# Third four of experts moved up, later down products behind their own up products, branch and row loads ahead of the last four

## Chip, cores, metric

One core of one Trainium2 chip. The metric is the device time of one execution in microseconds; three executions of the kernel before took 1126.81, 1130.20 and 1132.19 us (median 1130.2).

## The reference, cut to what matters

The program is one step of a two-layer backbone over 384 tokens of 1024 channels (128 context tokens, 256 latent ones). Each layer mixes tokens (convolution, windowed attention, spatial gating, one output projection) and then channels; each half ends in a LayerNorm. The change lies in the channel half, a mixture of experts in which every token takes 2 of 32 experts:

```python
gate = sum(one_hot(expert_id, 32) * top_w[..., None], axis=1)
hid = silu(einsum('td,edf->tef', t, w1)) * einsum('td,edf->tef', t, w3)
hid = hid * gate[..., None]
y = einsum('tef,efd->td', hid, w2)          # per expert 1024 -> 128 -> 1024
x = layer_norm(ALPHA * x + g2 * y, ln2_g, ln2_b)
```

## The kernel before, in words

`mixer` runs the token half, `moe` the channel half: `experts` (L1347), then `ln2` (L1679), once per layer. The 32 experts are taken in eight fours, `q` = 0 to 7. The 768 (token, expert) pairs are sorted by expert; matrix products with one-hot matrices (`gather_mm`) put the tokens' rows in that order, in three thirds of 256 places (`J` = 0, 1, 2; the third covers the later experts, the third four among them), and `evac` (L1356) copies a third from PSUM into `xT`.

For a four, `windows(q)` (L1367) copies 32 places for each of the four experts (ScalarE) and two further windows for experts with more rows (VectorE; the *second rows*). `ups(q, kqs)` (L1510) multiplies them with the up weights in four quarters `kq`; each quarter first copies the weights of the second rows' experts into `hv` (`copies`, L1392; two of three by VectorE, the third by ScalarE; two buffers) and ends in `self.done()`, which lets SP issue a later load into the freed buffer. `hidden` (L1420) applies SiLU on ScalarE and a product on VectorE, `hidden_T` (L1428) transposes the result on TensorE. `down(q, hT)` (L1466) makes the down products in three groups: two halves `z` = 0, 1 of the columns for the first rows, then both halves for the second rows. ScalarE scales `z` = 0 and the second rows by the gates, VectorE `z` = 1, and POOL writes the results into `y_d` in DRAM by one indirect DMA for the first rows (tile `ys`, two buffers) and one for the second rows (tile `ys2`, **one** buffer, so the second rows' scaling of the next four waits until this write has landed). The products go into the two PSUM banks of tag `sc`. Behind each write POOL does a piece of `affine`.

The gates and targets of these writes come from `gates` (L1201) and `slots` (L1279): some 25 small VectorE operations and twelve products. `overflow` (L1604) is a branch that runs only if an expert has more rows than the windows hold; on the given inputs it is not taken, but every engine loads `most` into a register and branches. `load_yy` (L1671) reads `y_d` back (three loads of 1 MB, a raw buffer each). The last four's down products (`down_keep`, L1482) stay in SBUF and are added up in token order by products with one-hot matrices (L1581, L1583); `ln2` adds the rows read back (L1691, first addition on PSUM at L1732) and normalizes.

Weights come in loads of 1 MB on SP's DMA queue: per four, four for the up products (32 per layer in ten buffers: tag `raw`, six, and `wx`, four) and two for the down products (`load_w2`, four buffers; issued behind the `down` that frees them). So a layer's fours load 48 MB.

The order on an engine named in `manual_schedule` is that of the code: VectorE, ScalarE and TensorE in the first block (L1515), TensorE alone in the second (L1546). Elsewhere a planner orders ScalarE, VectorE, POOL and SP by its own estimate of when each instruction is ready. It does not move instructions past the branch.

Of the kernel before, what the change touches and what calls it, by code (L numbers as in the profile page):

```python
# [8 lines left out]
F32 = mybir.dt.float32  # L9
# [11 lines left out]
D = 1024  # L21
NP, NS, T = 128, 256, 384
NT = 3
# [3 lines left out]
NQUAD = 8  # L27
# [52 lines left out]
class Kern:  # L80
# [1266 lines left out]
    def experts(self, l):  # L1347
        nc, mo, ep, tc = self.nc, self.mo, self.ep, self.tc
# [18 lines left out]
        def windows(q, ns=range(6)):  # L1367

            w = win[q]
            for n in ns:  # L1370
                at = first[4 * q + n] if n < 4 else more[q, n - 4]
                o, i_ = w[:, :, n * 32:(n + 1) * 32], xT[:, :, bass.ds(at, 32)]
                if n < 4:
                    self.act(o, i_, AF.Copy)
                else:
                    nc.vector.tensor_copy(o, i_)
            return w
# [42 lines left out]
        def hidden(ps):  # L1420

            pv = ps[:, 0:384].rearrange("p (h m f) -> p h m f", h=3, m=2)
            hid = ep.tile([128, 3, 64], F32, tag="hid", name="hid", bufs=1)
            self.act(hid, pv[:, :, 0, :], AF.Silu)
            nc.vector.tensor_tensor(hid, hid, pv[:, :, 1, :], op=ALU.mult)
            return hid
# [39 lines left out]
        def down(q, hT):  # L1466
            ys = self.eq.tile([128, D], F32, tag="ys", name="ys", bufs=2)
            yv = ys.rearrange("p (h z c) -> p h z c", h=2, z=2)
            for po, z in down_mm(q, hT):
                if z == 0:  # L1470
                    self.act(yv[:, :, 0, :], po.rearrange("p (h c) -> p h c", h=2), AF.Copy, scale=self.gate[:, 0, q:q + 1])
                elif z == 1:
                    nc.vector.tensor_scalar(yv[:, :, 1, :], po.rearrange("p (h c) -> p h c", h=2), self.gate[:, 0, q:q + 1], None, op0=ALU.mult)
                    scatter(self.y_d, ys, self.dst[:, 0, q:q + 1], 2 * T)
                else:
                    y2 = self.eq.tile([128, 512], F32, tag="ys2", name="ys2", bufs=1)
                    self.act(y2, po, AF.Copy, scale=self.gate[:, 1, q:q + 1])
                    scatter(self.y_d.rearrange("t (h c) -> (t h) c", h=2), y2, self.dst[:, 1, q:q + 1], 4 * T)
            for z in range(2):
                self.load_w2(l, 2 * q + z + 4)  # L1480
# [23 lines left out]
        w0 = ExitStack()  # L1504
# [5 lines left out]
        def ups(q, kqs):  # L1510
            for kq in kqs:
                up(ps[q], q, kq, win[q])

        ps = {}
        with tc.manual_schedule(engines={e.engine for e in (nc.vector, nc.scalar, nc.tensor)}):  # L1515

            for z in range(4):
                evac(0, z, "AAAV"[z])
            whos(0)
            windows(0)  # L1520
            ps[0] = self.bank("mm")
            ups(0, (0,))
            for z in range(4):
                evac(1, z, "AVAV"[z])
            ups(0, (1, 2, 3))
            windows(1)
            V.tensor_scalar(self.mid[:, 2, :], self.mid[:, 0, :], 1024.0, None, op0=ALU.add)
            ps[1] = self.bank("mm")
            ups(1, (0,))
            for i in range(NT):  # L1530
                self.onehot(oh[2, i], xT[:, i, 512:768], 2, i)
            self.gate_exp(self.logit)
            hid = hidden(ps[0])
            ups(1, (1,))
            hT = hidden_T(hid)
            ups(1, (2, 3))
            self.second_slots()
            whos(1)
            self.gates()
            for i in range(NT):  # L1540
                for part in (True, False):
                    self.gather_mm(oh, (2,), i, part)
        w0.close()
        self.eq = self.eqs.enter_context(tc.tile_pool(name=f"eq{l}", bufs=1, reuse_waits="tile"))

        with tc.manual_schedule(engines={nc.tensor.engine}):  # L1546
            self.slots()
            hid = hidden(ps[1])
            for z in range(4):
                evac(2, z, "AVAV"[z])  # L1550
            wn = self.hp.tile([128, 2, 8, 192], F32, tag="H", name="win")
            win += [wn[:, q % 2] for q in range(2, NQUAD)]
            windows(2)
            down(0, hT)
            for q in range(2, NQUAD):
                ps[q] = self.bank("mm")
                ups(q, (0, 1))
                hT = hidden_T(hid)
                ups(q, (2, 3))
                hid = hidden(ps[q])  # L1560
                if q < NQUAD - 1:
                    windows(q + 1)
                down(q - 1, hT)
            q, hT = NQUAD - 1, hidden_T(hid)
        self.ahead = self.NRAW
        self.overflow(l)
        self.load_yy(l)

        oT = [ep.tile([128, T], F32R, tag="hv", name="oT", bufs=2), self.eq.tile([128, 2, T], F32R, tag="ys", name="oT", bufs=2)]
        oT = [oT[0], oT[1][:, 0, :], oT[1][:, 1, :]]  # L1570
# [33 lines left out]
    def overflow(self, l):  # L1604
        nc, a, mo, ep, tc = self.nc, self.a, self.mo, self.ep, self.tc
        most = nc.values_load(self.most[0:1, 0:1], min_val=0, max_val=T + CAP + 6 * CAP * T)
        with tc.If(most > 2 * CAP):
            wo = self.wrp.tile([128, 2048], F32, tag="wr", name="wo")
            part = lambda c, n: wo[:, c:c + NT * n].rearrange("p (i e) -> p i e", i=NT)
# [26 lines left out]
            with tc.For_i(0, NQUAD, 1) as it:  # L1636
                nc.vector.tensor_copy(ixc, ix[:, :, bass.ds(it * 4, 4)])
                nc.vector.tensor_copy(gwc, gw[:, :, bass.ds(it * 4, 4)])
                w = [self.wx.tile([128, 2048], F32, tag="wx", name="w_ov") for _ in range(4)]
                for h in range(4):  # L1640
                    nc.sync.dma_start(w[h], a["w13"][bass.ds(it * 2 + (l * NHALF + h // 2), 1), h % 2].rearrange("o p c -> p (o c)"))
                w2 = [self.rawp.tile([128, 2048], F32, tag="raw", name="w2_ov") for _ in range(2)]
                for z in range(2):
                    nc.sync.dma_start(w2[z], a["w2"][bass.ds(it * 2 + (l * NHALF + z), 1)].rearrange("o p c -> p (o c)"))
                for e in range(4):
                    for i in range(NT):
                        ps = self.bank("mm")
                        for k in range(8):
                            c = e * 512 + k % 2 * 256
                            nc.tensor.matmul(ps[:, 0:256], tT[i][:, k * 128:(k + 1) * 128], w[k // 2][:, c:c + 256],  # L1650
                                             start=k == 0, stop=k == 7)
                        pv = ps[:, 0:256].rearrange("p (h m f) -> p h m f", h=2, m=2)
                        hid = ep.tile([128, 2, 64], F32, tag="hid", name="hidov", bufs=1)
                        self.act(hid, pv[:, :, 0, :], AF.Silu)
                        nc.vector.tensor_tensor(hid, hid, pv[:, :, 1, :], op=ALU.mult)
                        pt = self.bank("ms")
                        nc.tensor.transpose(pt[:, 0:128], hid.rearrange("p h f -> p (h f)"), self.ident)
                        hT = wo[:, 256:384]
                        nc.vector.tensor_copy(hT, pt[:, 0:128])
                        yo = wo[:, 1024:1024 + D]  # L1660
                        yv = yo.rearrange("p (h z c) -> p h z c", h=2, z=2)
                        for z in range(2):
                            po = self.bank("sc")
                            nc.tensor.matmul(po, hT, w2[z][:, e * 512:(e + 1) * 512], start=True, stop=True)
                            nc.vector.tensor_scalar(yv[:, :, z, :], po.rearrange("p (h c) -> p h c", h=2), gwc[:, i, e:e + 1], None, op0=ALU.mult)
                        nc.gpsimd.indirect_dma_start(
                            out=self.y_d, out_offset=bass.IndirectOffsetOnAxis(ap=ixc[:, i, e:e + 1], axis=0),
                            in_=yo, in_offset=None, bounds_check=2 * T - 1, oob_is_err=False)


    def load_yy(self, l):  # L1671
        nc = self.nc
        self.yy = []
        for i in range(NT):
            t = self.rawp.tile([128, 2, D], F32, tag="raw", name="yy")
            nc.sync.dma_start(t, self.y_d.rearrange("(c t) d -> t c d", c=2)[i * 128:(i + 1) * 128])
            self.yy.append(t)

    def ln2(self, l, ps):  # L1679
        nc, a, sm = self.nc, self.a, self.sm  # L1680
# [292 lines left out]
```

## Time and profile before

| | us |
|---|---|
| median of three executions | 1130.2 |
| the profiled execution, its own time | 1127.33 |
| its span, first to last instruction | 1125.6 |
| TensorE busy | 1011.2 |
| VectorE busy | 810.7 |
| ScalarE busy | 417.4 |
| POOL busy | 269.7 |

Busy times say little of a stage. The views used below are a table of stretches (busy time of each engine, granted TensorE clock as a share of full speed, share and rate of the DMA engines), the instructions of one engine in order of time (start, duration, engine, line, operation, out<-in, shape, count, in brackets the idle time before and what ended it), the DMA issues of a stretch with the time to landing, and the groups by line. Engines: PE is TensorE, PEld its weight loads, DVE VectorE, ACT ScalarE; a q marks an engine's sequencer. All times are from the start of the span. The experts of the first layer run from about 430 to 556 us, those of the second 545 us later.

### The profile page before, as it was taken

The numbers are of one execution on the slowest core, as the hardware profiler recorded it, in microseconds if no ns is written. First come the engines' busy times: TensorE is split into PE (matmuls) and PEld (weight loads), VectorE is DVE, ScalarE is ACT, GpSimd is POOL, SyncE is SP. The second block draws the span as 40 slices with busy tenths as digits, with TensorE's granted clock in tenths as the row PEclk, the third lists the DMA queues.
The fourth block names the chain that finished last, engine by engine and source line by source line (L and its number), as shares of the span: only waits on it lengthen the run. The fifth ranks groups of instructions, "written<-read, shape, count | busy, mean of one in ns | idle before, by whom it ended". The sixth has DMA issues, their size and how long they took to land. (4 is left out here: it accounts for less than half of the span.)

```text
span 1125.6 us, 20806 instructions
## 1 busy us (share of the span) xinstructions
PE 1011.2 (90%) x8182; PEld 840.7 (75%) x8182; DVE 810.7 (72%) x1530; ACT 417.4 (37%) x753; POOL 269.7 (24%) x232
## 2 busy tenths in 40 slices
PE   7999999999999999776689998999999999778673
PEld 5898978877999988433259897788999998754322
DVE  4399999965446986762569999997834587777437
ACT  4324254434333324341163443445532341434221
POOL 0001431221100510333244043114111025013335
PEclk9999999999999989897989999999999999989888
DMA  9967668447436667799585756773223666689955
GB/s 358 412 241 257 266 217 294 178 163 270 151 112 246 259 262 293 303 420 403 219 315 201 280 217 233 251 290 127 110 94 132 224 244 229 227 317 416 419 204 194
DMA packets 55101, 282.75 MB, mean 251 GB/s; under 512 B 8060, under 2 KB 12284, under 8 KB 27857
## 3 DMA queue, kind: packets, MB, share of 16 engines
q1 hardware_dynamic: 49632, 270.01, 63.1%
q0 software_dynamic: 5360, 11.29, 2.7%
q8 instruction: 69, 1.13, 0.4%
q14 instruction: 40, 0.32, 0.1%
HBM read 262.13 MB, written 24.71 MB: 255 GB/s over the span
## 5 line engine op out<-in xcount | busy, mean ns | idle before, releaser
L97 PE MATMUL ps_mm<-hThi,wr 128*128 128x384 f32 x672 | 229.9, 343 | 4.4 <-ACT hThi L102 2.3
L110 DVE TENSOR_TENSOR wr<-w_raw,wr 128x1024 fp32r<-128x1024 f32 x124 | 162.2, 1309 | 92.4 <-ACT wr L102 92.3
L98 PE MATMUL ps_mm<-hTlo,wr 128*128 128x384 f32 x672 | 228.0, 340 | 0.6 <-DVE hTlo L441 0.4
L99 PE MATMUL ps_mm<-hThi,wr 128*128 128x384 f32 x672 | 227.5, 339 | 0.6 <-DVE wr L110 0.6
L102 ACT ACTIVATE wr<-w_raw 128x1024 fp32r<-128x1024 f32 x140 | 147.5, 1055 | 68.1 <-PE ps_mm L99 37.8
L505 DVE SCALAR_TENSOR_TENSOR cacc<-pad,par,cacc 128x399 f32<-128x399 f32 x240 | 169.2, 705 | 4.2
L97 PEld LDWEIGHTS ps_mm<-hThi,wr 128*128 128x128 f32 x672 | 127.1, 189 | 18.2 <-issue 4.0
L98 PEld LDWEIGHTS ps_mm<-hTlo,wr 128*128 128x128 f32 x672 | 127.1, 189 | 6.3 <-DVE hTlo L441 2.5
L99 PEld LDWEIGHTS ps_mm<-hThi,wr 128*128 128x128 f32 x672 | 127.2, 189 | 2.5 <-DVE wr L110 0.9
L110 POOL TENSOR_TENSOR wr<-w_raw,wr 128x1024 fp32r<-128x1024 f32 x10 | 24.5, 2447 | 201.6 <-ACT wr L102 201.2
L1458 POOL DMA_INDIRECT y_d<-ys,dst x28 | 28.4, 1016 | 172.3 <-DVE hv L1400 73.3
L1446 PE MATMUL ps_sc<-w,hidT 128*32 128x512 f32 x256 | 43.1, 766 | 28.6 <-ACT ys L102 21.9
L1415 PE MATMUL ps_mm<-hv,win 128*32 128x128 f32 x1024 | 46.4, 277 | 9.2 <-DVE hv L1400 7.8
L1400 DVE COPY hv<-w_raw 128x512 f32 x60 | 41.9, 737 | 16.6 <-PE ps_mm L1415 10.8
L1415 PEld LDWEIGHTS ps_mm<-hv,win 128*32 128x32 f32 x1024 | 35.8, 112 | 22.7 <-DVE hv L1400 12.0
L1409 PE MATMUL ps_mm<-w_raw,win 128*32 128x256 f32 x640 | 47.8, 391 | 3.5 <-ACT win L102 3.5
L219 PE MATMUL ps_ms<-w_raw,cT 128*32 128x512 f32 x320 | 48.7, 612 | 1.4 <-DMA w_raw<-in_wada 1.4
L102 ACT ACTIVATE gate<-ps_mm 128x384 f32<-128x384 f32 x40 | 19.6, 490 | 81.6 <-PE ps_mm L99 80.5
L1446 PEld LDWEIGHTS ps_sc<-w,hidT 128*32 128x32 f32 x256 | 8.2, 123 | 45.8 <-ACT ys L102 32.9
L911 POOL TENSOR_TENSOR rtmp<-sc,lb 128x1024 f32<-128x1024 f32 x4 | 9.8, 2478 | 121.8 <-DMA lb<-in_ln 121.8
L842 POOL TENSOR_TENSOR merged<-merged,gate 128x384 f32<-128x384 f32 x16 | 18.1, 1135 | 87.0 <-DVE gate L841 87.0
L102 ACT ACTIVATE win<-xT 128x256 f32 x64 | 21.5, 409 | 37.6 <-PE ps_mm L1409 30.2
(505 smaller groups left out, 2355.7 us busy)
## 6 DMA issues: line engine op xcount, KB each, us to landing
w_raw<-in_wst SPq DMA_DIRECT2D x68, 1024.0 KB, 6.4
w_raw<-in_wada SPq DMA_DIRECT2D x48, 1024.0 KB, 5.4
w_raw<-in_w SPq DMA_DIRECT2D x40, 1024.0 KB, 10.7
w<-in_w SPq DMA_DIRECT2D x32, 1024.0 KB, 12.3
w_x<-in_w SPq DMA_DIRECT2D x24, 1024.0 KB, 11.8
bias<-in_bias SPq DMA_DIRECT2D x8, 768.0 KB, 7.6
y_d<-zero SPq DMA_DIRECT2D x2, 3072.0 KB, 15.1
yy<-y_d SPq DMA_DIRECT2D x6, 1024.0 KB, 7.1
```

Source lines behind the costliest of these rows:

```text
L97: mm(out, whi, xhi, start=first, stop=False)
L98: mm(out, whi, xlo, start=False, stop=False)
L99: mm(out, wlo, xhi, start=False, stop=last)
L102: return self.nc.scalar.activation(out, in_, f, **k)
L110: (eng or self.nc.vector).tensor_tensor(lo, x, hi.bitcast(F32), op=ALU.subtract)
L219: nc.tensor.matmul(ps[32 * t:32 * t + 32, :], self.cT[:, 2 * kp + k, :], w[:, t * 512:t * 512 + 512], start=(kp == 0 and k == 0), stop=(kp ...
L505: nc.vector.scalar_tensor_tensor(acc, pad[:, j:j + W], w, acc, op0=ALU.mult, op1=ALU.add)
L1400: nc.vector.tensor_copy(hv[:, i, :], src)
L1409: nc.tensor.matmul(ps[e * 32:(e + 1) * 32, 0:256], x[:, k, e * 32:(e + 1) * 32], w[:, e, kk, :], start=k == 0, stop=k == 7, skip_group_che ...
L1415: nc.tensor.matmul(ps[t * 32:(t + 1) * 32, 256:384], x[:, k, 128 + i * 32:160 + i * 32], hv[:, i, kk, h * 128:(h + 1) * 128], start=False, ...
L1446: nc.tensor.matmul(po[e * 32:(e + 1) * 32, :], hT[:, e * 32:(e + 1) * 32], w2[:, e, :], start=True, stop=True)
L1458: ins = nc.gpsimd.indirect_dma_start(out=view, out_offset=bass.IndirectOffsetOnAxis(ap=dst, axis=0), in_=rows, in_offset=None, bounds_chec ...
```

## The change

- The third four (`q` = 2) goes into the first block: the SiLU of the second four directly behind its up products, then after the last third's `gather_mm` the copies `evac(2)` and `windows(2)`, and all of `ups(2)`. `gates` and `slots` come behind it; in the second block `down(0)` and `down(1)` follow each other.
- `down(3)` and `down(4)` both follow `ups(4)`; from then on `down(q)` follows the up products of its own four, where it followed those of the next.
- `overflow` and `load_yy` stand ahead of `ups(7)`. The buffers of the rows read back are allotted before the branch, whose body borrows them. `ahead`, the number of up loads in flight, stays at ten until behind `ups(7)`.

```diff
             ups(1, (2, 3))
+            hid1 = hidden(ps[1])
             self.second_slots()
             whos(1)
-            self.gates()
             for i in range(NT):
                 for part in (True, False):
                     self.gather_mm(oh, (2,), i, part)
-        w0.close()
-        self.eq = self.eqs.enter_context(tc.tile_pool(name=f"eq{l}", bufs=1, reuse_waits="tile"))
-
-        with tc.manual_schedule(engines={nc.tensor.engine}):
-            self.slots()
-            hid = hidden(ps[1])
             for z in range(4):
                 evac(2, z, "AVAV"[z])
             wn = self.hp.tile([128, 2, 8, 192], F32, tag="H", name="win")
             win += [wn[:, q % 2] for q in range(2, NQUAD)]
             windows(2)
+            ps[2] = self.bank("mm")
+            ups(2, (0, 1))
+            hT1 = hidden_T(hid1)
+            ups(2, (2, 3))
+            self.gates()
+            w0.close()
+            self.eq = self.eqs.enter_context(tc.tile_pool(name=f"eq{l}", bufs=1, reuse_waits="tile"))
+            self.slots()
+
+        last = NQUAD - 1
+        with tc.manual_schedule(engines={nc.tensor.engine}):
+            hid = hidden(ps[2])
+            windows(3)
             down(0, hT)
-            for q in range(2, NQUAD):
+            down(1, hT1)
+            for q in range(3, last):
                 ps[q] = self.bank("mm")
                 ups(q, (0, 1))
-                hT = hidden_T(hid)
+                if q < 5:
+                    hT = hidden_T(hid)
                 ups(q, (2, 3))
                 hid = hidden(ps[q])
-                if q < NQUAD - 1:
-                    windows(q + 1)
-                down(q - 1, hT)
-            q, hT = NQUAD - 1, hidden_T(hid)
-        self.ahead = self.NRAW
+                windows(q + 1)
+                if q < 5:
+                    down(q - 1, hT)
+                if q >= 4:
+                    down(q, hidden_T(hid))
+
+        self.yy = [self.rawp.tile([128, 2, D], F32, tag="raw", name="yy") for _ in range(NT)]
         self.overflow(l)
         self.load_yy(l)
+        with tc.manual_schedule(engines={nc.tensor.engine}):
+            ps[last] = self.bank("mm")
+            ups(last, range(4))
+            q, hT = last, hidden_T(hidden(ps[last]))
+        self.ahead = self.NRAW
```

`overflow` takes its up weights from the three `yy` buffers and one more `raw` buffer, its down weights from two `wx` buffers; `load_yy` no longer allots.

## Rows read from the trace of the kernel before

**Rows 1.** Table of stretches, layer 0; columns in the first line

```profile
core 0: us, PE busy (x) PEld busy (x) DVE busy (x) ACT busy (x) POOL busy (x), PEclk, DMA share, GB/s
443.00:457.00 14.00, 9.21 (x88) 8.67 (x80) 9.85 (x37) 4.53 (x12) 0.00 (x0) 0.83 0.83 349
...
485.00:500.00 15.00, 11.17 (x214) 6.36 (x214) 9.15 (x17) 4.54 (x11) 5.56 (x5) 1.00 1.01 420
...
507.00:530.00 23.00, 14.43 (x189) 6.51 (x193) 6.56 (x16) 3.78 (x7) 7.67 (x5) 0.72 1.00 408
```

**Rows 2.** SP in order of time, layer 0

```profile
442.37 1.58 SPq L332 DMA_DIRECT2D w_x<-in_w  x2
...
459.33 2.08 SPq L342 DMA_DIRECT2D w<-in_w  x2
...
549.81 1.42 SPq L1676 DMA_DIRECT2D yy<-y_d  x3
```

**Rows 3.** DMA issues, 443.5 to 444 and 459.2 to 460 us; last: us to landing

```profile
w_x<-in_w SPq DMA_DIRECT2D x1, 1024.0 KB, 12.8
...
w<-in_w SPq DMA_DIRECT2D x1, 1024.0 KB, 4.9
```

**Rows 4.** Gates and slots, layer 0, DVE and PE in order of time

```profile
449.02 0.17 DVE L1205 TENSOR_REDUCE se<-ex 128x3 f32<-128x12 f32 x1 [1.69 <-issue]
...
454.63 2.77 PE L1304 MATMUL ps_ms<-V,RO 128*128 128x96 f32 x12 [4.79 <-ACT win L102]
```

**Rows 5.** ACT in order of time, layer 0, second rows' scaling among others

```profile
520.86 0.63 ACT L102 ACTIVATE hv<-w 128x512 f32 x1 [4.64 <-DMA w<-in_w]
...
521.39 0.67 ACT L102 ACTIVATE ys<-ps_sc,gate 128x512 f32<-128x512 f32 x1
...
538.52 0.69 ACT L102 ACTIVATE ys<-ps_sc,gate 128x512 f32<-128x512 f32 x1 [0.82 <-DMA y_d<-ys,dst]
...
545.07 0.69 ACT L102 ACTIVATE ys<-ps_sc,gate 128x512 f32<-128x512 f32 x1 [5.86 <-DMA y_d<-ys,dst]
```

**Rows 6.** Line 1458, writes into y_d, both layers

```profile
DMA to landing us min/median/max: 2.5/8.5/10.5
```

**Rows 7.** PE in order of time, layer 0, from the sixth four's down products

```profile
524.85 1.93 PE L1446 MATMUL ps_sc<-w,hidT 128*32 128x512 f32 x8 [0.81 <-ACT ys L102]
...
529.37 1.72 PE L1409 MATMUL ps_mm<-w_x,win 128*32 128x256 f32 x16
...
532.76 0.33 PE L1430 MATMUL ps_ms<-con,hid 128*128 128x128 f32 x1
...
535.90 1.04 PE L1446 MATMUL ps_sc<-w,hidT 128*32 128x512 f32 x8
...
539.70 1.07 PE L1453 MATMUL ps_sc<-hv,hidT 128*32 128x256 f32 x16 [0.88 <-DVE ys L1473]
...
544.15 3.60 PE L1446 MATMUL ps_sc<-w,hidT 128*32 128x512 f32 x16 [2.86 <-PEq L1607]
...
551.27 0.50 PE L1583 MATMUL ps_tp<-ysk,oT 128*128 128x512 f32 x1 [0.29 <-DVE ysk L1494]
```

**Rows 8.** Group by line, both layers: product of hidden

```profile
L1425 DVE TENSOR_TENSOR hid<-hid,ps_mm 128x192 f32<-128x192 f32 x16 | 5.6, 351 | 10.9 <-ACT hid L102 10.8
```

**Rows 9.** Line 1607, the branch, both layers: ns min/median/max, first and last start

```profile
L1607 SPq EVENT_SEMAPHORE  x14: 17/17/17, 538.2 to 1083.4; - x14
...
L1607 PEldq COMPARE_BRANCH  x2: 3342/3381/3420, 540.4 to 1085.8; - x2
```

**Rows 10.** DVE in order of time, layer 0, LayerNorm

```profile
555.59 0.69 DVE L1732 TENSOR_TENSOR x<-ps_tp,yy 128x512 f32<-128x512 f32 x1
...
558.53 1.75 DVE L1691 TENSOR_TENSOR yy<-yy 128x512 f32<-128x512 f32 x1
560.20 2.28 DVE L1701 SCALAR_TENSOR_TENSOR x<-r,x 128x1024 f32<-128x1024 f32 x1
...
567.36 1.22 DVE L1701 SCALAR_TENSOR_TENSOR x<-r,x 128x1024 f32<-128x1024 f32 x1
```

More of the change, by code (lines that the diff above doesn't have):

```diff
@@ L1606, in overflow @@
         most = nc.values_load(self.most[0:1, 0:1], min_val=0, max_val=T + CAP + 6 * CAP * T)
+        spare = self.rawp.tile([128, 2048], F32, tag="raw", name="w_ov")
+        w = [t.rearrange("p c d -> p (c d)") for t in self.yy] + [spare]
+        w2 = [self.wx.tile([128, 2048], F32, tag="wx", name="w2_ov") for _ in range(2)]
         with tc.If(most > 2 * CAP):
@@ L1638, in overflow @@
                 nc.vector.tensor_copy(gwc, gw[:, :, bass.ds(it * 4, 4)])
-                w = [self.wx.tile([128, 2048], F32, tag="wx", name="w_ov") for _ in range(4)]
                 for h in range(4):
                     nc.sync.dma_start(w[h], a["w13"][bass.ds(it * 2 + (l * NHALF + h // 2), 1), h % 2].rearrange("o p c -> p (o c)"))
-                w2 = [self.rawp.tile([128, 2048], F32, tag="raw", name="w2_ov") for _ in range(2)]
                 for z in range(2):
@@ L1672, in load_yy @@
         nc = self.nc
-        self.yy = []
         for i in range(NT):
-            t = self.rawp.tile([128, 2, D], F32, tag="raw", name="yy")
-            nc.sync.dma_start(t, self.y_d.rearrange("(c t) d -> t c d", c=2)[i * 128:(i + 1) * 128])
-            self.yy.append(t)
+            nc.sync.dma_start(self.yy[i], self.y_d.rearrange("(c t) d -> t c d", c=2)[i * 128:(i + 1) * 128])
     def ln2(self, l, ps):
```

## The prediction

> **What bounds the kernel now.** I read the table of stretches first. Between 485 and 500 us the DMA engines' share is 1.01 at 420 GB/s, and it is 1.00 from 507 to 530 [rows 1]: no engine is as full, so most of the experts' time is the stream of weights, and a 1 MB load costs 1.049 MB / 420 GB/s = 2.5 us. Changing the order of products there pays nothing. Three places of a layer aren't of that kind.
>
> *The hole at the front.* From 443 to 457 the share is only 0.83 [rows 1]. SP issues two up loads at 442.37, then nothing until down weights at 459.33 [rows 2]. The later of the two takes 12.8 us, so lands at 456.4; the down load takes 4.9 and lands at 464.2 [rows 3]. Without a gap it would land at 458.9: **5.3 us of stream are lost**, since SP waits for `down(0)`, and that for gates and slots (VectorE from 449.02, TensorE's L1304 at 454.63 after waiting 4.79) [rows 4].
>
> *The chain behind the last up weights but one.* The down weights of the sixth four land at 520.8; ScalarE copies `hv` from them at once [rows 5]. The DMA binds up to here and no further: SP's first record behind its wait for the last loads is at 538.2 [rows 9], while the first addition of `ln2` waits until 555.59 [rows 10]. In between, TensorE runs the rest of `down(5)` from 524.85, `ups(7)` from 529.37, `down(6)` from 535.90, the branch, then `down_keep` from 544.15 [rows 7]. Beside it runs a second chain: the second rows' scalings on ScalarE at 521.39, 538.52 and 545.07 (a fourth at about 530, as the spacing of 8.5 asks) each wait for the previous write to land [rows 5]; then the last write, then SP's reading back at 549.81 [rows 2]. Both chains end within a few us of each other, at 555.59.
>
> *LayerNorm*, 13.0 us from 555.59 to 568.58, the end of its last sum (567.36 + 1.22) [rows 10].
>
> **The change part by part**, for one layer; the second repeats the first 545 us later. No bytes, products or branches are added or dropped.
>
> *Third four moved up.* Its up products free buffers, so four up loads now follow at 456.4 without waiting for gates. Behind them the down loads still wait for `down(0)`, now behind `ups(2)`, gates and slots. `ups` cost 6.0 (529.37 to 535.90 less 0.52 of transposes, judged by the 0.33 of one [rows 7]), and I add 2.3 for `evac` and `windows` ahead of them, about half the wait of 4.79 [rows 4]: 8.3. L1304 comes at 463, the load is issued at 467.6 and lands at 472.5. Gapless it would be 456.4 + 5 x 2.5 = 468.9, so 3.6 stay lost of 5.3: **-1.7**. Bounds: -5.3, if slots come 3.6 earlier than that; +2.4, if the wait of 4.79 comes whole and VectorE's gates start late by as much as their chain lasts (5.6, 449.02 to 454.63), 4.1 beyond my sum.
>
> *`down` of neighbouring fours back to back* (0 and 1, 3 and 4). The second's second rows wait for the first's write through the one `ys2`: 8.5 by the median landing [rows 6]. ScalarE's later window copies stand behind that. In the streaming stretch TensorE is busy 11.17 of 15 us, ScalarE 4.54 [rows 1]: one such wait is covered by the stream, since ten up loads are ahead. Taken at 0; without that cover up to 8.5, once.
>
> *`down(6)` behind its own up products, and ahead of the branch and `ups(7)`.* TensorE's order after the landing at 520.8 becomes: rest of `down(5)`, 4.5 (524.85 to 529.37); `ups(6)`, 6.0; waiting for `hidden` and transposes, which before lay between quarters, 1.9 (0.52, three elementwise steps at about 0.35 [rows 8], handoffs); `down(6)` 3.8 (535.90 to 539.70); the last second-row products and branch, 4.45 (539.70 to 544.15); `ups(7)` 6.0 and again 1.9; from `down_keep` to the last L1583 of the first token tile 7.6 before (544.15 to 551.77), less 1.5, since its 16 products took 3.60 where twice eight should take 2 x 1.04 [rows 7] with no standstill ahead of them: 6.1. Sum 34.65, against 555.59 - 520.86 = 34.7, which before held 3.8 of waiting for the rows read back: **0**. Bounds: `down(5)` 3.0 and `down(6)` 2.1 where no bank is waited for (-3.2); `down(5)` whole at 8.6 (520.8 to 529.4), `down_keep` still 7.6 (+5.6).
>
> *Branch.* It takes 3.34 to 3.42 us on TensorE's sequencer [rows 9], and stays. The Trainium skill ("Advanced Engine Details and Errata", Control Flow Timing) gives about 108 ns for a compare-and-branch; by it the step would be some 3.2 us cheaper per layer. No row supports that, and the measurement decides. New is what waits at the branch: SP for outstanding loads (538.2 [rows 9]), POOL for its writes. `ups(7)`'s copies on ScalarE and VectorE stand behind their own branches.
>
> *Rows read back.* They move past the last up products but not past SP's wait for all loads: issue at about 537 to 541, in place of 549.81 [rows 2]. Three loads, landing over the next 10 us, beside `ups(7)` and `down_keep`: hidden. What they postpone on SP is the next layer's first tiles, which before stood behind them as well. Uncovered they would cost what they cost now. The pair sums on VectorE (1.75 each, L1691) then run before the first addition, where before two stood inside `ln2`, and the last sums fall from 2.28 toward 1.22 without the traffic beside them [rows 10]: of 13.0 us I take off one pair, 1.75, and 1.06: **-2.8**. Bounds: 0, and both pairs, -3.5.
>
> Sum per layer -1.7 + 0 - 2.8 = -4.5; two layers **-9.0**. The profiled execution took 1127.33, 2.9 below the median of three; 1130.2 - 9.0 = **1121.2**. About 0.5% (5.65 us) is what a measurement of this kernel tells from no change.
>
> **Rivals.** *A, stronger gain.* The stream closes up (-5.3 for -1.7) or no `down` waits for a bank (-3.2 for 0): -8.1 or -7.7 per layer, about 1114; both together -11.3, so 1107.6. For it: the front hole is due to waits, not work. Against: the new order keeps the down loads behind slots.
>
> *B, the second chain takes the first's place and nothing is won.* The second rows' writes aren't shortened: they still come one at a time, 8.5 apart [rows 5]. `down(6)`'s scaling now stands ahead of ScalarE's branch, and behind that come the copies and SiLU for `ups(7)`. If four scalings are still pending at 520.8, it comes at 545.07 as before, ends at 545.76, and `ups(7)` and the rest (6.0 + 1.9 + 6.1 = 14.0) end at 559.8: +4.2, less 2.8 and 1.7 is -0.3 per layer, so 1126 to 1134. For it: the spacing, and that no buffer is added. Against: `down(3)` to `down(5)` are issued earlier, so the queue should be one shorter. The point from which it binds is a scaling at about 540.8 (540.8 + 0.7 + 14.0 = 555.5, my chain's end); each us later costs one.
>
> *C, slower.* The chain of B, one step longer: `down`s that are neighbours put two scalings on the one `ys2` in a row, and ScalarE, held by the second, delays its window copies and the next four. One more step of 8.5 puts the scaling for `down(6)` at 553.6 and the first addition at 568.3: +12.7, less 2.8 and 1.7 is +8.2 per layer, about 1147. Before, the same wait (5.86 at 545.07 [rows 5]) lay beside TensorE's branch, with `ups(7)` long done; now `ups(7)` is behind it, so nothing is left to cover it. Against: `down(5)` still starts at the same landing, and writes can land in 2.5 [rows 6]. The Trainium skill ("DMA: Bandwidth & Descriptors", Issuing engines are not separate DMA queues) says that transfers of all engines run on the same 16 DMA engines and interleave, so a write moved into the stream isn't fast. The trace agrees, as landings spread from 2.5 to 10.5 us [rows 6].
>
> *D, reading back not earlier.* If SP's wait holds the three loads until the last write lands, at 549, the pair sums stay where they are: -2 per layer at best, which lies within B's band.
>
> **How the numbers follow.** My forecast (-5 to -14 in all) 0.45; A (-14 to -23) 0.15; B with D 0.22; C 0.18. Faster by over 0.5% is A and the forecast without its small end (0.05): 0.15 + 0.40 = 0.55; within 0.5% is that end with B and D: 0.27; slower is C: 0.18. The range runs from A's 1107 to 1139, half of C's way, which leaves out C's full price, a tenth at most, and little else. The likeliest case alone spans 1116 to 1126.
>
> **What would show it.** Right: DMA share from 443 to 470 above 0.9, the first down load issued near 467.6, the fifth four's earlier end by 1.7; SP reading back before 542; TensorE's `ups(7)` starting near 538 to 541 and following the branch by under 1 us; first addition about 34.7 behind the landing of the sixth four's down weights; LayerNorm near 10.2. Wrong: ScalarE's scaling for `down(6)` after 540 with a wait on `y_d`, and TensorE idle behind the branch for `hv` or for `hidden`; a hole at the front above 5.3; or L1732 waiting for `yy`.

## The result, and the profile after

The changed kernel takes 1145.84 us (median of four, 1142.69 to 1146.49) against 1129.95 beside it: ratio 1.0128, interval 1.0092 to 1.0164, **slower by 1.3%**. The profiled execution's span grew from 1125.6 to 1144.7.

Where it went, by the first layer's marks: ScalarE's copy at the landing of the sixth four's down weights, the first addition of `ln2`, the end of the last LayerNorm sum. They stood at 520.86, 555.59, 568.58 and stand at 520.29, 564.96, 583.63. So the landing is 0.6 earlier, the chain behind it 44.7 in place of 34.7, LayerNorm 18.7 in place of 13.0. In the second layer the landing is 9.6 later (1065.74 to 1075.37), the chain 45.7 against 34.8, LayerNorm 10.9 against 12.3. Of the 15.05 lost in the first layer 5.4 were given back up to the second's landing; the chain behind it added 10.9.

The stream first, stretches as in [rows 1]. The second stretch before:

```profile
457.00:485.00 28.00, 25.65 (x412) 13.62 (x412) 22.36 (x56) 11.06 (x23) 13.38 (x10) 0.90 0.87 342
```

The same stretches after, and SP's first down loads in them:

```profile
443.00:457.00 14.00, 11.73 (x140) 10.35 (x134) 6.95 (x27) 4.55 (x12) 0.00 (x0) 0.88 0.79 331
457.00:485.00 28.00, 19.98 (x297) 11.94 (x291) 20.44 (x60) 6.67 (x13) 9.04 (x6) 0.82 0.92 353
...
507.00:530.00 23.00, 13.87 (x193) 6.22 (x197) 9.95 (x17) 4.76 (x11) 9.04 (x7) 0.75 0.98 398
```

```profile
461.47 0.33 SPq L342 DMA_DIRECT2D w<-in_w  x1
...
464.66 10.81 SPq L342 DMA_DIRECT2D w<-in_w  x3
```

The hole has moved rather than closed: the DMA share is 0.79 where it was 0.83, and 0.92 in the next stretch where it was 0.87.

ScalarE in order of time, the rows that answer to [rows 5]; the scalings at 516.35, 533.07, 543.98 and 547.58 are those of second rows:

```profile
516.35 0.68 ACT L102 ACTIVATE ys<-ps_sc,gate 128x512 f32<-128x512 f32 x1
520.29 0.63 ACT L102 ACTIVATE hv<-w 128x512 f32 x1 [3.26 <-DMA w<-in_w]
524.66 0.69 ACT L102 ACTIVATE ys<-ps_sc,gate 128x512 f32<-128x512 f32 x1 [3.75 <-PE ps_sc L1446]
530.27 0.63 ACT L102 ACTIVATE hv<-w_raw 128x512 f32 x1 [4.92 <-PE ps_sc L1453]
532.53 0.63 ACT L102 ACTIVATE hv<-w_x 128x512 f32 x1 [1.63 <-PE ps_mm L1415]
533.07 0.67 ACT L102 ACTIVATE ys<-ps_sc,gate 128x512 f32<-128x512 f32 x1
...
543.98 0.67 ACT L102 ACTIVATE ys<-ps_sc,gate 128x512 f32<-128x512 f32 x1
547.58 0.69 ACT L102 ACTIVATE ys<-ps_sc,gate 128x512 f32<-128x512 f32 x1 [2.93 <-DMA y_d<-ys,dst]
```

One scaling is done before the landing, as I had said, but the next isn't 8.5 behind it: ScalarE's order has two weight copies ahead of it, and the first waits 4.92 for products of `down(5)`. The last waits for the write before it to land (2.93). TensorE beside it, answering to [rows 7]:

```profile
521.28 0.47 PE L1430 MATMUL ps_ms<-con,hid 128*128 128x128 f32 x1 [5.98 <-DVE hid L1425]
...
522.67 1.93 PE L1446 MATMUL ps_sc<-w,hidT 128*32 128x512 f32 x8 [0.51 <-issue]
525.40 1.94 PE L1446 MATMUL ps_sc<-w,hidT 128*32 128x512 f32 x8 [0.80 <-ACT ys L102]
528.22 1.94 PE L1453 MATMUL ps_sc<-hv,hidT 128*32 128x256 f32 x16 [0.88 <-DVE ys L1473]
529.92 1.93 PE L1409 MATMUL ps_mm<-w_raw,win 128*32 128x256 f32 x16
...
538.30 1.06 PE L1446 MATMUL ps_sc<-w,hidT 128*32 128x512 f32 x8 [0.51 <-issue]
540.17 1.06 PE L1446 MATMUL ps_sc<-w,hidT 128*32 128x512 f32 x8 [0.80 <-ACT ys L102]
542.11 1.07 PE L1453 MATMUL ps_sc<-hv,hidT 128*32 128x256 f32 x16 [0.88 <-DVE ys L1473]
548.46 1.93 PE L1409 MATMUL ps_mm<-w_x,win 128*32 128x256 f32 x16 [5.28 <-ACTq L1627]
...
558.06 1.92 PE L1446 MATMUL ps_sc<-w,hidT 128*32 128x512 f32 x16 [0.46 <-DVE hidT L1436]
...
564.31 0.50 PE L1600 MATMUL ps_tp<-ysk,oT 128*128 128x512 f32 x1 [0.28 <-DVE ysk L1494]
```

Each group of `down(5)` and `down(6)` waits until the one before it has been evacuated (0.80, 0.88): one of the two PSUM banks of `sc` is held by second rows not yet scaled. The 5.28 ahead of `ups(7)` is put down to ScalarE's sequencer at the branch, which ScalarE reaches only behind its scaling at 547.58. TensorE's own branch was over at 546.3 (542.8 and 3.48, last fences below), and it stood on for 2.

SP and POOL, then VectorE in LayerNorm (to be held against [rows 2, 10]):

```profile
548.54 0.98 POOL L1458 DMA_INDIRECT y_d<-ys,dst  x1 [2.64 <-ACTq L1627]
...
552.39 2.76 SPq L1692 DMA_DIRECT2D yy<-y_d  x3
```

```profile
564.96 0.69 DVE L1747 TENSOR_TENSOR x<-ps_tp,yy 128x512 f32<-128x512 f32 x1
565.85 0.69 DVE L1747 TENSOR_TENSOR x<-ps_tp,yy 128x512 f32<-128x512 f32 x1 [0.20 <-PE ps_tp L1600]
572.44 0.17 DVE L546 TENSOR_SCALAR chb<-par 128x8 f32<-128x8 f32 x1 [5.89 <-DMA par<-in_par]
...
582.40 1.23 DVE L1716 SCALAR_TENSOR_TENSOR x<-r,x 128x1024 f32<-128x1024 f32 x1
```

The rows are read back at 552.39, later than 549.81: the loads stand ahead of `ups(7)` in the code, and wait for the last write all the same. In LayerNorm VectorE stands 5.89 on the next layer's parameters. Their buffer is the one of the transposed hidden rows, which `down_keep` now reads later, and the planner put their first use in the middle of LayerNorm. In the traces read below it did so wherever the branch stands ahead of `ups(7)`, and nowhere else.

### The profile page after: what moved, and what is told of

Read it like the earlier page. It is cut to its first block, busy times and chain, and to the rows that moved or that the text cites. A ratio compares the mean times of both kernels' runs of the same rounds, so it can differ in the third digit from the quotient of the medians.

```text
span 1144.7 us, 20816 instructions
## 1 busy us (share of the span) xinstructions
PE 1010.5 (88%) x8182; PEld 846.4 (74%) x8182; DVE 805.7 (70%) x1530; ACT 417.2 (36%) x753; POOL 264.6 (23%) x232
## 5 line engine op out<-in xcount | busy, mean ns | idle before, releaser
L1458 POOL DMA_INDIRECT y_d<-ys,dst x28 | 28.1, 1003 | 177.1 <-ACT hv L102 90.3
L1415 PE MATMUL ps_mm<-hv,win 128*32 128x128 f32 x1024 | 51.5, 289 | 10.7 <-DVE hv L1400 10.6
L1415 PEld LDWEIGHTS ps_mm<-hv,win 128*32 128x32 f32 x1024 | 40.9, 118 | 25.1 <-DVE hv L1400 14.6
L1446 PE MATMUL ps_sc<-w,hidT 128*32 128x512 f32 x256 | 38.8, 695 | 17.9 <-ACT ys L102 8.2
L1400 DVE COPY hv<-w_raw 128x512 f32 x60 | 33.4, 597 | 27.0 <-PE ps_mm L1415 20.7
L1409 PE MATMUL ps_mm<-w_x,win 128*32 128x256 f32 x384 | 33.5, 444 | 15.0 <-ACTq L1627 10.5
L219 PE MATMUL ps_ms<-w_raw,cT 128*32 128x512 f32 x320 | 44.9, 611 | 1.3 <-DMA w_raw<-in_wada 1.3
L1400 DVE COPY hv<-w 128x512 f32 x48 | 29.4, 644 | 9.5 <-PE ps_mm L1415 3.6
```

Of the source, the lines that this page charges most:

```text
L219: nc.tensor.matmul(ps[32 * t:32 * t + 32, :], self.cT[:, 2 * kp + k, :], w[:, t * 512:t * 512 + 512], start=(kp == 0 and k == 0), stop=(kp ...
L1400: nc.vector.tensor_copy(hv[:, i, :], src)
L1409: nc.tensor.matmul(ps[e * 32:(e + 1) * 32, 0:256], x[:, k, e * 32:(e + 1) * 32], w[:, e, kk, :], start=k == 0, stop=k == 7, skip_group_che ...
L1415: nc.tensor.matmul(ps[t * 32:(t + 1) * 32, 256:384], x[:, k, 128 + i * 32:160 + i * 32], hv[:, i, kk, h * 128:(h + 1) * 128], start=False, ...
L1446: nc.tensor.matmul(po[e * 32:(e + 1) * 32, :], hT[:, e * 32:(e + 1) * 32], w2[:, e, :], start=True, stop=True)
L1458: ins = nc.gpsimd.indirect_dma_start(out=view, out_offset=bass.IndirectOffsetOnAxis(ap=dst, axis=0), in_=rows, in_offset=None, bounds_chec ...
```

## The experiments

All ratios are to the kernel before, run beside them on the same chip.

**The two halves of the change.** `e1_front` has the new first block and the old rest, `e2_tail` the reverse:

```diff
...
             down(0, hT)
+            down(1, hT1)
-            for q in range(2, NQUAD):
+            for q in range(3, NQUAD):
```

> Only the first part of the change: the third four in the first block; down products, branch and row loads as in the kernel before. Theory T (the loss is TensorE's work that now stands behind the landing of the sixth four's down weights): the landing comes 0.6 us earlier per layer as in the changed kernel and the rest is as before, so 1126 to 1131, not slower. Rival W (one buffer for the second rows' results: their writes come one at a time and hold ScalarE at the branch): the same, 1126 to 1131. Rival F (the front is at fault: gates and slots now come later and the stream of weights loses more than it gains): 1138 to 1146.

1127.26 us, 0.9984 (0.9964 to 1.0004).

> Only the rest of the change: first block as before, then the new order of the down products, branch and row loads ahead of the last up products. Theory T and rival W: the whole loss is here, 1143 to 1149. Rival F: 1128 to 1134.

1144.26 us, 1.0141 (1.0110 to 1.0172). The loss is in the second half; the front gives nothing that can be told from noise. F falls.

**Two buffers for the second rows' results**, in the changed kernel (and two for the tile `V` of `slots`, which shares the tag):

```diff
-y2 = self.eq.tile([128, 512], F32, tag="ys2", name="ys2", bufs=1)
+y2 = self.eq.tile([128, 512], F32, tag="ys2", name="ys2", bufs=2)
```

> The changed kernel with two buffers for the second rows' results, so that no scaling waits for the write before it. Theory T: TensorE's own chain stays; the last up products start at the end of TensorE's branch, 546.4 instead of 548.5 in layer 0, and the row loads some 3 us earlier: 2 to 3 us per layer, 1139 to 1143. Rival W: the whole loss of about 8 us per layer goes, 1127 to 1133.

1125.49 us, 0.9970 (0.9943 to 0.9998): by the ratios **1.6%, some 18 us, less than with one buffer**, a little past W's number. The landing on ScalarE, then TensorE, same products as above:

```profile
518.63 0.63 ACT L102 ACTIVATE hv<-w 128x512 f32 x1 [6.26 <-DMA w<-in_w]
```

```profile
516.23 1.93 PE L1446 MATMUL ps_sc<-w,hidT 128*32 128x512 f32 x8 [2.82 <-DMA w<-in_w]
518.66 1.48 PE L1446 MATMUL ps_sc<-w,hidT 128*32 128x512 f32 x8 [0.50 <-DMA w<-in_w]
...
520.81 1.05 PE L1409 MATMUL ps_mm<-w_raw,win 128*32 128x256 f32 x16
...
528.09 1.92 PE L1446 MATMUL ps_sc<-w,hidT 128*32 128x512 f32 x16 [0.46 <-DVE hidT L1436]
529.96 1.07 PE L1453 MATMUL ps_sc<-hv,hidT 128*32 128x256 f32 x16
534.57 1.94 PE L1409 MATMUL ps_mm<-w_x,win 128*32 128x256 f32 x16 [3.53 <-PEq L1627]
```

and its SP and VectorE:

```profile
539.62 2.65 SPq L1692 DMA_DIRECT2D yy<-y_d  x3
```

```profile
551.79 0.69 DVE L1747 TENSOR_TENSOR x<-ps_tp,yy 128x512 f32<-128x512 f32 x1
```

No bank is waited for, the stand ahead of `ups(7)` is TensorE's own branch (3.53, from PEq), the rows are read back at 539.62, and the first addition comes 33.2 behind the landing. The edit also let the planner order VectorE anew: it now forms the hidden product at 512.40, ahead of the copies, where in the changed kernel it came at 520.88, behind them. What part of the 18 us that is wasn't separated.

**One four more of delay** (`down(5)` behind `ups(6)`), first with one buffer:

```diff
-                if q < 5:
-                    hT = hidden_T(hid)
+                hT = hidden_T(hid)
...
-                if q < 5:
-                    down(q - 1, hT)
-                if q >= 4:
+                down(q - 1, hT)
+                if q == last - 1:
                     down(q, hidden_T(hid))
```

> The changed kernel, but down products stay one four behind until the seventh: down(4) behind ups(5), down(5) and down(6) both behind ups(6), branch and row loads still ahead of ups(7). Theory T: ups(6), 6.4 us, and the 1.9 us for its hidden rows go back ahead of the landing, so the last up products start 6 to 8 us earlier per layer and the kernel takes 1129 to 1135. Rival W: the scalings of the second rows still come one at a time and the last of them, which ScalarE's branch waits for, stays near 547 in layer 0: 1142 to 1149.

1139.55 us, 1.0093 (1.0066 to 1.0119): between the two theories. The last scaling of the first layer came at 548.44, as W said. The first addition came at 566.22, 1.3 later than in the changed kernel, and at 1114.18 in the second layer, 6.9 earlier. ScalarE's copy for `down(6)` waited 6.24 for its weights: the edit delays their load as well, so it separates T from W only in part.

**Two buffers without the change, and with its front alone:**

> The kernel before the change with two buffers for the second rows' results. Theory W (an unscaled set of second rows holds one of the two PSUM banks of the down products and its write holds the row loads): before the change too the writes, one at a time, set the issue of the row loads at 549.8; without that the first addition comes when TensorE is ready, 551.8 instead of 555.6, or earlier by what the banks gave: 4 to 6 us per layer, 1118 to 1123. Rival T (TensorE's chain behind the landing set the end before the change): 1127 to 1131.

1115.43 us, 0.9869 (0.9838 to 0.9900).

> The third four moved up as in the change, everything else as in the kernel before, with two buffers. Theory W: what two buffers give to the kernel before, and the 0.3 us to 1.2 us per layer of the front on top: 1116 to 1122. Rival T: 1126 to 1130.

1114.29 us, 0.9860 (0.9828 to 0.9891): not to be told from `b2_two`, and faster than both kernels. The one buffer held the kernel before too, by 1.3%; its TensorE waited 6.30 ahead of the sixth four's down products, for the scaling at 521.39 [rows 5] to free a bank:

```profile
522.11 1.93 PE L1446 MATMUL ps_sc<-w,hidT 128*32 128x512 f32 x8 [6.30 <-ACT ys L102]
```

But with two buffers the changed order is still 1.1% behind `f2_front_two`, some 12 us: a second cost, that no buffer explains. T was half right. ScalarE, TensorE and VectorE of `f2_front_two`:

```profile
520.46 0.63 ACT L102 ACTIVATE hv<-w 128x512 f32 x1 [3.57 <-DMA w<-in_w]
```

```profile
523.04 1.95 PE L1409 MATMUL ps_mm<-w_x,win 128*32 128x256 f32 x16
...
530.15 1.04 PE L1446 MATMUL ps_sc<-w,hidT 128*32 128x512 f32 x8
533.10 1.07 PE L1446 MATMUL ps_sc<-w,hidT 128*32 128x512 f32 x8 [1.91 <-DMA w<-in_w]
...
539.63 3.39 PE L1446 MATMUL ps_sc<-w,hidT 128*32 128x512 f32 x16 [3.70 <-PEq L1615]
```

```profile
548.41 1.29 DVE L1740 TENSOR_TENSOR x<-ps_tp,yy 128x512 f32<-128x512 f32 x2
```

At 523.04 the *last* up products start, not those of the seventh four; the first addition is at 548.41, 28.0 behind the landing at 520.46.

**Where the branch stands**, with one buffer and with two: `overflow` and `load_yy` put back behind `ups(7)`.

> The changed kernel with branch and row loads behind ups(7), at the place they had; down products in the new order, one buffer. Theory W with the branch as carrier (ups(7) waits for ScalarE, which reaches its branch only behind the last second-row scaling): ups(7) starts near 543.5 instead of 548.5 in layer 0, TensorE's branch of 3.4 us comes behind it, so 1 to 3 us per layer come back: 1139 to 1144. Theory W with the bank alone as carrier (one of two banks held): ups(7) needs no such bank and the end is set by the writes and row loads as now: 1144 to 1148.

1143.59 us, 1.0108 (1.0065 to 1.0151).

> The changed kernel with two buffers, branch and row loads behind ups(7), where they were before the change; down products in the new order. Theory U: the order of the down products costs, the branch's place doesn't: 1123 to 1128. Rival B: 1112 to 1118.

1125.05 us, 0.9970 (0.9951 to 0.9990), as U said. With two buffers the place makes no difference, and one buffer costs 1.4% here, 1.6% there. So holding ScalarE at the branch is not the whole of W; with one buffer and the branch behind `ups(7)` the chain is still 45.6 and 41.3.

Set side by side, the runs with the third four moved up separate the two costs:

| ratio to the kernel before | one buffer | two buffers |
|---|---|---|
| old order of the down products | 0.9984 (`e1_front`) | 0.9860 (`f2_front_two`) |
| new order, branch behind `ups(7)` | 1.0108 (`e5_late`) | 0.9970 (`e12_two_late`) |
| new order, branch ahead of it (the change) | 1.0128 | 0.9970 (`e4_two`) |

The second buffer is worth 1.2 to 1.6% in each order, which the intervals don't tell apart. The new order costs 1.1% with two buffers and 1.2 to 1.4% with one. So most of what the change lost, some 12 us, is its order, and the one buffer at most added a little to that. `e12_two_late` differs from `f2_front_two` in the order of the down products (with their loads) and in when the buffers of the rows read back are allotted. In the first layer its landing is at 522.28 and its first addition at 556.03, 33.8 behind it in place of 28.0.

**More delay, with two buffers** (the edit of `e3_lag` and two buffers):

> The changed kernel with two buffers for the second rows' results, and down products one four behind until the seventh (down(5) and down(6) both behind ups(6)); branch and row loads ahead of ups(7). Measured so far in layer 0, from the landing of the sixth four's down weights to the first addition: 44.7 us changed, 33.2 changed with two buffers, 28.0 third four moved up with two buffers. Theory U (down products behind their own up products put ups(6) and the wait for its hidden rows, 8 us, behind this landing): 26 to 29 us here, the kernel at 1112 to 1118. Rival B (the branch and the row loads ahead of ups(7) are what costs): 32 to 34 us as with the changed order, 1121 to 1126.

1124.66 us, 0.9988 (0.9970 to 1.0007). U's number isn't reached, but by the trace not for B's reason (the profiled execution took 1135.96, 11.3 above the median):

```profile
533.10 1.94 PE L1446 MATMUL ps_sc<-w,hidT 128*32 128x512 f32 x8 [5.54 <-DMA w<-in_w]
536.21 1.94 PE L1446 MATMUL ps_sc<-w,hidT 128*32 128x512 f32 x8 [1.17 <-DMA w<-in_w]
...
542.28 1.94 PE L1409 MATMUL ps_mm<-w_x,win 128*32 128x256 f32 x16 [2.43 <-PEq L1625]
```

`down(6)` now waits for its own weights, which are loaded behind a later `down`, and has nothing beside that wait. The edit moved loads as well as products, so it doesn't test U cleanly.

**Without the branch**, two buffers (what experts with more rows need is left out):

> The changed kernel with two buffers and without the branch: the code for experts with more rows than the windows hold is left out altogether. TensorE's wait of 3.5 us per layer ahead of ups(7) goes. If that chain sets the end of both layers, 7 us less than with the branch: 1116 to 1120. If something beside it is as late (row loads, the writes), 1122 to 1126.

1113.54 us, 0.9872 (0.9846 to 0.9897): by the ratios 11 us, with an interval of some 7 to 15. In `e4_two` TensorE stood 3.53 at the first layer's branch and 5.92 at the second's, 9.5 in all. The chain is 28.6 and 28.1, as short as in `f2_front_two`. In the first layer, though, the first addition comes at 551.15, hardly before that of `e4_two` (551.79), since the landing is 3.9 later; what is gained there lies in LayerNorm, which takes 11.3 in place of 19.1 without the wait for parameters. What the old order would gain without its branch wasn't run. Its TensorE behind `down(6)`:

```profile
535.82 1.07 PE L1453 MATMUL ps_sc<-hv,hidT 128*32 128x256 f32 x16
537.07 0.86 PE L1415 MATMUL ps_mm<-hv,win 128*32 128x128 f32 x14 [0.19 <-DVE hv L1400]
...
537.87 1.03 PE L1409 MATMUL ps_mm<-w_x,win 128*32 128x256 f32 x14
```

With no branch to stop it, the planner drew the first quarter of `ups(7)` into `ups(6)`, and the rest runs on at once at 1.03 for 14 (granted clock 1.00 of full speed), where behind the branch 16 took 1.94 (0.50).

**The wait for the parameters.**

> The changed kernel with two buffers, and the one small VectorE operation that reads the next layer's parameters (line 546) held until layer 0's last LayerNorm square is issued. Theory P: VectorE stands 6.1 us in the middle of LayerNorm for the landing of these parameters, and that is lost outright: 1118 to 1121. Rival Q: the next layer waits for its first weights anyway and gives it back: 1123 to 1127.

1125.02 us, 0.9957 (0.9933 to 0.9980): inconclusive, since the operation still stood inside LayerNorm, waiting 4.36; the edit tied an operation of VectorE to one of ScalarE. `e5_late` says more: its LayerNorm took 11.3 without such a wait, so that VectorE's same instructions were 6.2 earlier than in the changed kernel near 598 us, and only 1.0 near 852. What this wait costs was mostly given back; why the token half gives back isn't settled.

**ScalarE in the order of the code** in the second block, one buffer:

```diff
-with tc.manual_schedule(engines={nc.tensor.engine}):
+with tc.manual_schedule(engines={nc.tensor.engine, nc.scalar.engine}):
```

> The changed kernel with one buffer, ScalarE in the order of the code from down(0) to ups(6), so that each second-row scaling stands directly behind its down products and ahead of later weight copies. Theory W1 (the writes' landing times alone set the chain, some 9 us a step): the scaling of the fifth four comes near 526 instead of 533 in layer 0, the last near 544 instead of 547.6, ups(7) starts at the end of TensorE's branch, and the kernel takes 1138 to 1142. Theory W2 (ScalarE is held either way: a scaling that waits for a write now holds the weight copies of the next up products, and TensorE with them): no gain, 1144 to 1152. If the place on ScalarE were the whole loss, 1123 to 1128, as with two buffers.

1138.71 us, 1.0060 (1.0036 to 1.0084), W1's number. The execution with the trace took 2459.16 us and isn't read, so that W1's times of the single scalings stay unseen. By the ratios some 8 of the 18 us (3 to 12 by the intervals) are the planner's place for the scalings; that the rest goes with the landing of the writes is W1's argument, and not shown.

## Why the prediction was wrong

*Stream:* forecast -1.7, measured -0.6 in the first layer, and `e1_front` shows no gain. That the down loads wait for gates and slots was wrong: the first two were issued at 461.47 and 464.66 (forecast 467.6), ahead of L1304 at 465.51, since the planner had put `down(0)`'s first products at 441.55. Only the next loads came behind it, at 474.24. The upper bound of this part is mis-added as well: the two delays that it names, 2.5 and 5.6, make 8.1 and not 4.1; no other number hangs on it.

*TensorE's chain behind the landing:* my terms beside the changed kernel and `e4_two`, first layer, from starts in the two traces:

| | forecast | changed | two buffers |
|---|---|---|---|
| rest of `down(5)` | 4.5 | 9.6 | 2.2 |
| `ups(6)` and its hidden rows | 7.9 | 8.4 | 7.3 |
| `down(6)` and branch | 8.25 | 10.2 | 6.5 |
| `ups(7)` and its hidden rows | 7.9 | 9.6 | 10.3 |
| `down_keep` to the last L1600 of the first tile | 6.1 | 6.8 | 6.8 |
| sum | 34.65 | 44.5 | 33.0 |

With two buffers the sum comes near, by luck: `down(5)` and `down(6)` are shorter than forecast by 4.1 together, and `ups(7)`, whose first products run at the lower clock, is longer by 2.4. With one buffer the terms that fail most are `down(5)`, `down(6)` with the branch, and `ups(7)`. The 4.5 for `down(5)` is its length from 524.85 [rows 7], while the landing was at 520.86 and TensorE needed 8.5 from it. That half of `down(5)` is done by then is true only, as in `e4_two` (516.23), when no bank is held and VectorE's hidden product isn't queued behind copies of the same weights (TensorE idle 5.98). My upper bound held "`down(5)` whole at 8.6"; the middle value was the error.

*The step that failed* is the third part (`down(6)` behind its own up products), put at 0 by "Sum 34.65, against 555.59 - 520.86 = 34.7": the chain behind the landing measured 44.7 against 34.7, and 45.7 against 34.8 in the second layer. It failed on both sides of the comparison.

*The new order's side* is "Taken at 0" for `down` of neighbouring fours, with the choice between B and C. I had the place, the price (1147; measured 1145.84) and the deciding point (a scaling later than 540.8; measured 547.58), and gave C 0.18, because the queue of scalings would be one shorter. It was. But the steps between scalings were 16.7, 10.9 and 3.6 in place of 8.5: a step takes a write's landing at the least, and ScalarE's own queue comes on top. That C's price came so near is luck: C had the last scaling at 553.6, the first addition at 568.3 and a shorter LayerNorm, where 547.58, 564.96 and a longer one were measured.

*The old order's side* weighs more. I took 34.7, with 3.8 of waiting in it, for what the old order needs. It needs 28.0 to 30.0 (`f2_front_two`, `b2_two`), the rest was the one buffer. Against that the changed order lost some 5 us in the first layer even with no scaling held up (33.2 and 33.8): `ups(6)`, `ups(7)` and a wait for hidden rows behind each stand behind the landing, where the old order has `ups(7)` alone and runs it while the next down weights load. That the order costs is shown by the table of ratios; that it costs by these products, and not by its loads, is read from the traces, and the runs meant to test it (`e3_lag`, `e10_two_lag`) moved loads too.

*Rows read back:* 537 to 541 forecast, 552.39 measured; D was right in that the loads wait for the last write. With two buffers, 539.62. *LayerNorm:* -2.8 forecast; -1.4 in the second layer; +5.7 in the first, by the parameters, which I hadn't looked for although the shared buffer is in the code.

*Branch:* TensorE's compare and branch took 3.48 to 3.74 us (its sequencer's rows of line 1627). The Trainium skill ("Advanced Engine Details and Errata", Control Flow Timing) gives about 108 ns. No run here shows that on TensorE, and the measurement decides; on the other engines the same branch took 0.05 to 0.07 us. Writes beside the weight loads landed late: that of 528.91 took 9.7, those of 544.92 and 548.54, behind the last load, 2.6 and 2.8; over both layers 2.5 to 9.9, median 7.5. That agrees with the Trainium skill ("DMA: Bandwidth & Descriptors", Issuing engines are not separate DMA queues), by which transfers of all engines interleave on the same 16 DMA engines. The rows:

```profile
L1627 PEldq COMPARE_BRANCH  x2: 3483/3612/3740, 542.8 to 1098.5; - x2
```

```profile
DMA to landing us min/median/max: 2.5/7.5/9.9
```

## What to carry over

Before an order is changed, find out what the present order would take without the wait that now hides it: here a second buffer of a little over 2 KB per partition was worth 1.3%, more than any order tried, and worth about as much in the new order as in the old. A result that leaves through a single buffer makes a chain of landings, and every engine queue in which its evacuation stands adds to it. What stands behind the last landing is to be short: products moved behind their own inputs gain nothing if the engine then has to wait for each step.

## What was unexpected of the hardware

What a branch costs may go beyond its own 3.5 us: without it the changed order with two buffers gained some 11 us (7 to 15), where TensorE had stood 9.5 at it, so that a cost beyond the stand isn't shown. Behind the stand of 3.53 the next 16 up products took 1.94 at a granted clock of 0.50 of full speed (1.2 GHz), the last 16 of `ups(7)` 1.05 at 1.00 (2.4 GHz). How much of the 11 that is, how much the quarter of `ups(7)` drawn ahead, and how much the wait for parameters in LayerNorm, wasn't separated.
